# A one-core decoder block: the largest top-k search taken off VectorE, two merged operands in slots, the mixer products one block later

## The chip, the cores and the metric

The kernel runs on one core of one Trainium2 chip. The metric is the device time of one execution in microseconds (us). TensorE (PE in the profile) multiplies and transposes, VectorE (DVE), ScalarE (ACT) and GpSimd (POOL) do the elementwise work, and SyncE (SP) issues the DMAs.

## The reference, cut to what matters

One decoder layer on x of 1024 tokens by 1024 features in float32. Three sub-layers follow one another, each between two RMS norms and added to the residual; the change touches the first, the mixer.

```python
proj = h @ w_in          # pool channels | q | k | v | index q, k, weights | two gates
a   = _pool_mixer(u_pool, pool_w, pool_scale) @ w_proj_pool
att = _sparse_attention(q, k, v, q_idx, k_idx, w_idx, rel_bias_table)
merged = sigmoid(g_pool) * a + sigmoid(g_attn) * (att @ w_proj_attn)
return merged @ w_out
```

The pool mixer takes trailing means over 2, 4, 8 and 16 tokens in four groups of 128 channels, minus the token, and multiplies each group by a 128x128 matrix. The sparse attention scores all keys for each query with four small index heads, keeps the 256 best causal keys of each query, and does softmax attention over those in eight heads. Then follow attention over 256 memory tokens and a SwiGLU network of width 2816.

## The kernel before, in words

Tokens come in eight blocks of 128. Every float32 product is done as three products of rounded operands: `split` rounds a tile to its high part on ScalarE and subtracts to get the low part on VectorE (names with h and l, as `h_wq`, `l_wq`). So each weight tile and each operand costs one ScalarE and one VectorE instruction before TensorE can use it.

Nothing is issued in the order in which it is written. A `Recorder` collects all instructions of the program with their dependences, gives each a cost (`_cost`), and `schedule` builds each engine's order by a greedy simulation: at each step, an engine that is free takes the earliest-written instruction among those that are ready, and a hand-over from one engine to another is counted as `HOP` = 190 ns. The engines then run these fixed orders, each instruction behind the one before it. Where the real durations differ from `_cost`, an engine waits at the head of its queue for what the plan took to be ready. Buffers are counted too: 42 slots of 4 KB per partition (tag "b"), 4 load buffers (tag "ld"), 3 raw weight buffers ("wraw"), 2 each for the high and low weights ("whi", "wlo"), 4 single PSUM banks and 2 double ones. Instructions that allocate a slot may not run more than 700 instructions ahead of the oldest one that is still to do.

The stages of the mixer, with their span in the profile, are these. Norm and transposition of x, index projections, and scores of the query blocks 2 to 7 (`do_scores`, to 85 us; blocks 0 and 1 need no choice). The four groups of the pool mixer (`for g in range(4)`, from about 60 us to 137 us): two half products `o_u`, trailing sums on GpSimd (`us`), their difference to the token on VectorE (`pl`), split into `ph` and `pll`, two products `mx` with the group's matrix, split into `mh` and `ml`. Then eight blocks m of 128 columns of the pool gate (`for m in range(KC)`, to 255 us): for each half of the tokens a gate product `o_gp`, a tanh on ScalarE, and the projection `ap` of the four mixer results. Then keys, values, queries (`o_k`, `o_v`, `o_q`, to 367 us), two blocks of the attention gate (`o_ga`), keys and values of the memory (`km`, `vm`, from 388 us), attention unit by unit (`lg`, `pt`, `po`), the output projection `o_pa` of the attention in two halves of the tokens (`proj_attn`, the second half to 708 us), and the product with `w_out` (`y`, from 708 us).

The search for the 256 best keys (`topk`) is a bitwise search for a threshold, 32 rounds long. In a round each query block (384 to 1024 keys wide) is compared with its current threshold and counted in one VectorE instruction (`tja`, output bf16, with a sum); then two small instructions on all blocks' counts (`reja`, `canda`) give the next threshold. After the last round, each block needs seven VectorE instructions (`gt`, `left`, `eq`, `pre`, `eq`, `gt`, `mask`) for the exact mask. `topk` is a generator: `tick` moves it on by a third of a round's blocks or so from places in the loops over pool groups, gates, keys, queries, and `tick(1000)` behind the memory's keys and values writes what is left. That sets only the place in the written order, so the rank among ready instructions.

`proj_attn` writes the merged halves to DRAM (`mgd`) through load buffers `gt`; `merged(b)` reads a block of 128 tokens back into a load buffer `mg` and splits it into `mgh` and `mgl` for `y`. The first two blocks' operands `ym` are written behind the whole second half of `proj_attn`.

Of the kernel before, what the change touches and what calls it, by code (L numbers as in the profile page):

```python
# [10 lines left out]
F32 = mybir.dt.float32  # L11
F32R = mybir.dt.float32r
# [5 lines left out]
P = 128  # L18
S = 1024
# [34 lines left out]
class Recorder:  # L54
# [130 lines left out]
    def _cost(self, eng, name, args, kw):  # L185
        n = self._free(args[0])
        src = args[1] if len(args) > 1 and self._is_ap(args[1]) else args[0]
        big = max(n, self._free(src))
        if name == "dma_start":
            a = args[0]  # L190
            total = 1
            for st, c in list(a.ap):
                total *= c
            return (60.0 if eng == "sync" else 1000.0), total * 4 / 360.0
        if eng == "tensor":
            if name == "transpose":
                return 109.0, 0.0
            return n * 0.43 + 7.0, 0.0
        if eng == "scalar":
            return 150 + 0.89 * big + (190 if kw.get("accum_out") is not None else 0), 0.0  # L200
        if eng == "vector":
            ps = any(self.tiles.get(a.tensor.name, [""])[0].startswith("ps") for a in args if self._is_ap(a))
            fast = name in ("tensor_copy", "tensor_scalar", "tensor_single_scalar") and not ps
            if kw.get("accum_out") is not None:
                return 280 + 1.05 * big, 0.0
            return 130 + (0.56 if fast else 1.06) * big, 0.0
        if name == "tensor_scalar":
            return 195 + 1.0 * n, 0.0
        if name == "tensor_copy":
            return 60 + 3.4 * n, 0.0  # L210
        if name == "memset":
            return 60 + 1.0 * n, 0.0
        if kw.get("op") == OP.pow:
            return 464.0, 0.0
        return 60 + 2.1 * n, 0.0
# [125 lines left out]
def hybrid_block_kernel(ctx: ExitStack, tc: tile.TileContext, x, mem, norm_mix_pre, norm_mix_post,  # L341
# [12 lines left out]
    def slot(shape, dt, name):  # L354
        return nc.tile(sb, shape, dt, name=name, tag="b", bufs=NSLOT)
# [286 lines left out]
                                fill=LOW, base=0, channel_multiplier=1)  # L642


    def topk(blocks, tag):
        nb = len(blocks)
        cnt = nc.tile(sb, [P, nb], F32, name=f"cnt{tag}", tag=f"cnt{tag}")
        rej = nc.tile(sb, [P, nb], I32, name=f"rej{tag}", tag=f"rej{tag}")
        cand = [nc.tile(sb, [P, nb], I32, name=f"cand{tag}{j}", tag=f"cand{tag}{j}") for j in range(2)]
        for rnd in range(32):  # L650
            cur = cand[rnd % 2]
            for a, i in enumerate(blocks):
                n = (i + 1) * P
                thr = 0.0 if rnd == 0 else cur[:, a:a + 1].bitcast(F32)
                junk = nc.tile(sb, [P, S], BF, name=f"tj{tag}{rnd}{i}", tag="bf", bufs=2)
                nc.vector.tensor_scalar(junk[:, :n], score[i][:, :n], thr, None, op0=OP.is_ge, op1=OP.add,
                                        accum_out=cnt[:, a:a + 1])
                if a % 3 == 2:
                    yield
            bit = -1 if rnd == 0 else 1 << (31 - rnd)  # L660
            nxt = 1 << (30 - rnd) if rnd < 31 else 0
            nc.vector.tensor_scalar(rej, cnt, float(TOPK), float(bit), op0=OP.is_lt, op1=OP.mult)
            if rnd == 0:
                nc.vector.tensor_single_scalar(cand[1], rej, nxt, op=OP.bitwise_xor)
            else:
                nc.vector.scalar_tensor_tensor(cand[(rnd + 1) % 2], rej, nxt, cur,
                                               op0=OP.bitwise_xor, op1=OP.bitwise_xor)
        fin = cand[0]
        for a, i in enumerate(blocks):
            n = (i + 1) * P  # L670
            thr = fin[:, a:a + 1].bitcast(F32)
            sc = score[i]
            gt = nc.tile(sb, [P, S], BF, name=f"gt{i}", tag="bf", bufs=2)
            nc.vector.tensor_scalar(gt[:, :n], sc[:, :n], thr, None, op0=OP.is_gt, op1=OP.add,
                                    accum_out=cnt[:, a:a + 1])
            left = small([P, 1], F32, f"left{i}")
            nc.vector.tensor_scalar(left, cnt[:, a:a + 1], -1.0, float(TOPK), op0=OP.mult, op1=OP.add)
            eq = nc.tile(sb, [P, S], BF, name=f"eq{i}", tag="bf", bufs=2)
            nc.vector.tensor_scalar(eq[:, :n], sc[:, :n], thr, None, op0=OP.is_equal)
            pre = slot([P, S], F32, f"pre{i}")  # L680
            nc.vector.tensor_tensor_scan(pre[:, :n], eq[:, :n], eq[:, :n], 0.0, op0=OP.add, op1=OP.max)
            nc.vector.scalar_tensor_tensor(eq[:, :n], pre[:, :n], left, eq[:, :n], op0=OP.is_le, op1=OP.mult)
            nc.vector.scalar_tensor_tensor(gt[:, :n], eq[:, :n], -1.0, gt[:, :n], op0=OP.add, op1=OP.add)
            nc.vector.tensor_scalar(mask(i), gt[:, :n], -NEG, None, op0=OP.mult)
            yield

    bg = {"gen": None}

    def tick(n=1):
        for _ in range(n):  # L690
            if bg["gen"] is not None and next(bg["gen"], "end") == "end":
                bg["gen"] = None

    for i in range(2, NB):
        do_scores(i)
    bg["gen"] = topk([2, 3, 4, 5, 6, 7], "a")


    rc = nc.tile(sb, [P, 16], F32, name="rc", tag="rc")
# [2 lines left out]
    pwr = wload(pool_w.rearrange("g c d -> c g d"), "pw")  # L702
    pwh, pwl = slot([P, 4, P], F32R, "pwh"), slot([P, 4, P], F32R, "pwl")
    split(pwh, pwl, pwr)
    mixh, mixl = [], []
    for g in range(4):
        w = WINDOWS[g]
        wh, wl = wcols(w_in, C_POOL + g * P, f"wu{g}", keep=True)
        uu = slot([P, S], F32, f"uu{g}")
        for h in range(2):  # L710
            o = gemm_half(wh, wl, hT, h, f"u{g}", (0, 512) if g or h else (0, 256, 512))
            nc.scalar.activation(uu[:, h * 512:(h + 1) * 512], o, AF.Copy)
            tick(1)
        a, st = uu, 1
        while st < w:
            b_ = slot([P, S], F32, f"us{g}{st}")
            nc.gpsimd.tensor_copy(b_[:, :st], a[:, :st])
            nc.gpsimd.tensor_tensor(b_[:, st:], a[:, st:], a[:, :S - st], op=OP.add)
            a, st = b_, st * 2
        nc.gpsimd.tensor_tensor(a[:, :w], a[:, :w], rc[:, :w], op=OP.mult)  # L720
        nc.gpsimd.tensor_scalar(a[:, :w], a[:, :w], float(w), None, op0=OP.mult)
        pl = slot([P, S], F32, f"pl{g}")
        nc.vector.scalar_tensor_tensor(pl, a, 1.0 / w, uu, op0=OP.mult, op1=OP.subtract)
        ph, pl_ = slot([P, S], F32R, f"ph{g}"), slot([P, S], F32R, f"pll{g}")
        split(ph, pl_, pl)
        mh, ml = slot([P, S], F32R, f"mh{g}"), slot([P, S], F32R, f"ml{g}")
        for h in range(2):
            s = slice(h * 512, (h + 1) * 512)
            o = bank([P, 512], f"mx{g}{h}")
            mm3(o, pwh[:, g], pwl[:, g], ph[:, s], pl_[:, s], True, True)  # L730
            split(mh[:, s], ml[:, s], o, scale=pscale[:, g:g + 1])
        mixh.append(mh)
        mixl.append(ml)


    span = 383
# [26 lines left out]

    mAd = nc.tile(dr, [KC, P, S], F32, name="mAd", tag="mAd", dram=True)
    sAd = nc.tile(dr, [KC, P, S], F32, name="sAd", tag="sAd", dram=True)
    for m in range(KC):
        if m % 2 == 0:
            v = w_proj_pool.rearrange("(k p) n -> p k n", p=P)[:, :, m * P:(m + 2) * P]
# [2 lines left out]
        mA = slot([P, S], F32, f"mA{m}")  # L771
        for h in range(2):
            s = slice(h * 512, (h + 1) * 512)
            o = gemm_half(wh, wl, hT, h, f"gp{m}")
            nc.scalar.activation(mA[:, s], o, AF.Tanh, scale=0.5)
            o2 = bank([P, 512], f"ap{m}{h}")
            cs = slice((m % 2) * P, (m % 2 + 1) * P)
            for c in range(4):
# [253 lines left out]
    for k, (u, nxt) in enumerate(zip(units, units[1:] + [None])):  # L1032
# [4 lines left out]
            attn_gate(k + GFIRST - 1)  # L1037
        for m in PROJ.get(k, ()):
            proj_attn(0, [m], wide=k == 15)
    proj_attn(1, range(KC))  # L1040


    x1d = nc.tile(dr, [S, D], F32, name="x1d", tag="x1d", dram=True)
    x2d = nc.tile(dr, [S, D], F32, name="x2d", tag="x2d", dram=True)
    def merged(b):
        mg = nc.tile(sb, [P, KC, P], F32, name=f"mg{b}", tag="ld", bufs=LD)
        nc.sync.dma_start(mg, mgd[:, :, b * P:(b + 1) * P].rearrange("k d t -> d k t"))
        mgh, mgl = slot([P, KC, P], F32R, f"mgh{b}"), slot([P, KC, P], F32R, f"mgl{b}")
        split(mgh, mgl, mg, scale=0.5)
        return lambda c: (mgh[:, c], mgl[:, c])  # L1050

    ym = [merged(b) for b in range(2)]
    wo = [wsplit(wload(w_out[c * P:(c + 1) * P, :], f"wo{c}"), f"wo{c}", keep=True) for c in range(KC)]
    g2, g3 = gain(norm_mix_post, "g2"), gain(norm_mem_pre, "g3")
    h2T = QuartT("h2")
# [365 lines left out]
```

## Time and profile before

| | us |
|---|---|
| median of three runs (lowest, highest) | 1581.72 (1580.98, 1583.4) |
| the profiled execution | 1580.3 |
| its span on the core | 1578.5 |

Mean granted clock of the profiled execution: 0.996 of full speed. TensorE is busy over 1540.6 us of the span, VectorE over 1100.4, ScalarE over 594.7, GpSimd over 214.9. A busy time is the union of the instructions' spans; a matmul's recorded span is longer than the distance to the next one's start, so a stretch in which TensorE is fully busy can still be slow, and the granted clock has to be read beside it.

### The profile page before, as it was taken

To read this page: it belongs to the slowest core of one execution; us is meant where nothing else is said; L and a number is where in the kernel's file an instruction comes from. 1 tells how busy PE (TensorE), PEld (TensorE's weight loads), DVE (VectorE), ACT (ScalarE), POOL (GpSimd) and SP (SyncE) were. 2 spreads that over 40 slices of the span, in tenths; PEclk is the share of its full clock that TensorE was granted. 3 is DMA by queue.
4 is the path that set the end of the run, shared out by engine and by line. 5 is a ranking of instruction groups with operands and counts; after the bars stand their busy time and mean duration, and the time that the engine had idled before them with its cause. 6 is when DMAs were issued, how large, how long until landed. Compare 5 with 4: busy or idle time off the path is not lost.

```text
span 1578.5 us, 20510 instructions
## 1 busy us (share of the span) xinstructions
PE 1540.6 (98%) x7458; PEld 1294.1 (82%) x7458; DVE 1100.4 (70%) x1848; ACT 594.7 (38%) x991; POOL 214.9 (14%) x311
## 2 busy tenths in 40 slices
PE   6999999999999999999999999999999999999998
PEld 6877888887888888887799887888888888888886
DVE  5699888889743686556865676776677776665545
ACT  6532111222443565324545663222222331464431
POOL 6055000001122442001212220000000000000002
PEclk9999999999999999999999999999999999999999
DMA  7322412453833222489973527644444443786654
GB/s 223 72 67 64 130 54 67 124 183 127 247 101 94 81 74 81 138 273 353 387 272 124 205 83 276 213 157 161 166 164 162 154 153 127 245 292 195 219 175 160
DMA packets 213781, 262.20 MB, mean 166 GB/s; under 512 B 11944, under 2 KB 144816, under 8 KB 213680
## 3 DMA queue, kind: packets, MB, share of 16 engines
q1 hardware_dynamic: 213680, 260.89, 50.6%
q8 instruction: 59, 0.97, 0.3%
q14 instruction: 42, 0.34, 0.1%
HBM read 177.47 MB, written 83.63 MB: 165 GB/s over the span
## 4 chain that ended last, share of the span: by engine, by line
PE 83%; DVE 7%; issue 3%; DMA 3%; ACT 2%; POOL 1%; SPq 0%; DVEq 0%; POOLq 0%; ACTq 0%
PE gb L139 11%; PE gc L139 8%; PE ga L139 7%; PE dB L139 6%; PE o_q L139 5%; PE y L139 5%; PE o_gp L139 5%; PE o_ga L139 4%; PE dA L139 4%; PE o_pa L139 4%; PE dC L139 3%; PE po L139 3%; PE lg L139 3%; PE qm L139 3%; PE z L139 3%
## 5 line engine op out<-in xcount | busy, mean ns | idle before, releaser
L139 DVE TENSOR_SCALAR_CACHE_REDUCE tja<-score,canda 128x384 bf16<-128x384 f32 (+1 forms) x186 | 165.5, 941 | 0.8
L139 DVE TENSOR_TENSOR dlP<-drP,dhP 128x1024 fp32r<-128x1024 f32 x77 | 93.8, 1224 | 49.7 <-ACT dhP L139 27.7
L139 ACT ACTIVATE dhP<-drP 128x1024 fp32r<-128x1024 f32 x77 | 81.6, 1061 | 73.7 <-DMA drP<-wdnT 22.6
L139 POOL TENSOR_SCALAR mef<-ms,ms 128x1 f32<-128x1 f32 x8 | 3.8, 472 | 611.0 <-ACT jf L139 610.7
L139 POOL TENSOR_SCALAR L<-L,ri 128x256 f32<-128x256 f32 (+7 forms) x64 | 47.9, 751 | 162.1 <-DVE ri L139 143.6
L139 ACT ACTIVATE h<-s 128x1024 fp32r<-128x1024 f32 x44 | 45.7, 1056 | 63.1 <-DVE s L139 25.9
L139 PE MATMUL lg<-kTh,qq 128*128 128x512 f32 (+2 forms) x192 | 59.1, 353 | 0.8 <-DVE nn L139 0.8
L139 DVE TENSOR_TENSOR l<-s,h 128x1024 fp32r<-128x1024 f32 x44 | 53.6, 1218 | 5.0 <-PE gc L139 4.8
L139 DVE CUSTOM_DVE_ANT_0 L<-lg,mb 128x256 f32<-128x256 f32 (+1 forms) x64 | 25.1, 400 | 44.9 <-PE lg L139 42.6
L139 DVE TENSOR_TENSOR T<-pt,T 128x512 fp32r<-128x512 f32 x72 | 47.6, 685 | 12.5 <-ACT T L139 12.4
L139 PE MATMUL po<-T,Vh 128*128 128x512 f32 x144 | 54.4, 407 | 1.3 <-DVE T L139 0.8
L139 PE MATMUL y<-h_wo,mgh 128*128 128x512 f32 x128 | 50.9, 398 | 2.4 <-ACT mgh L139 2.4
L139 ACT ACTIVATE T<-pt 128x512 fp32r<-128x512 f32 x72 | 40.4, 595 | 33.4 <-PE pt L139 32.9
L139 POOL TENSOR_TENSOR mb<-Bn,mask 128x1024 f32<-128x1024 f32 (+1 forms) x16 | 33.5, 2092 | 138.9 <-DVE gt L139 115.6
L139 PE MATMUL o_ga<-hTh,h_wga 128*128 128x512 f32 x128 | 50.2, 392 | 1.4 <-DVE Vml__670 L139 1.4
L139 PE MATMUL dB<-dhP 128*128 128x512 f32 x132 | 51.3, 389 | 0.0
L139 PE MATMUL dB<-dlP,dhP 128*128 128x512 f32 x132 | 51.3, 389 | 0.0
L139 PE MATMUL dB<-dhP,dlP 128*128 128x512 f32 x132 | 51.3, 389 | 0.0
L139 PE MATMUL y<-h_wo,mgl 128*128 128x512 f32 x128 | 49.9, 396 | 1.4 <-DVE mgl L139 1.4
L139 PE MATMUL y<-l_wo,mgh 128*128 128x512 f32 x128 | 50.6, 395 | 0.0
L139 PE MATMUL o_pa<-ath,h_wpa 128*128 128x512 f32 x128 | 50.5, 395 | 0.0
L139 PE MATMUL o_pa<-ath,l_wpa 128*128 128x512 f32 x128 | 50.2, 392 | 0.0
(429 smaller groups left out, 4824.8 us busy)
## 6 DMA issues: line engine op xcount, KB each, us to landing
uw<-unitd SPq DMA_DIRECT2D x28, 512.0 KB, 7.0
r_wg<-in_w_gate_up_dram SPq DMA_DIRECT2D x22, 512.0 KB, 5.6
r_wu<-in_w_gate_up_dram SPq DMA_DIRECT2D x22, 512.0 KB, 5.5
r_wdr<-in_w_down_dram SPq DMA_DIRECT2D x22, 512.0 KB, 4.2
wdnT<-r_wdr SPq DMA_DIRECT2D x44, 256.0 KB, 4.5
actS<-gv SPq DMA_DIRECT2D x44, 256.0 KB, 4.8
drP<-actS SPq DMA_DIRECT2D x44, 256.0 KB, 3.8
drP<-wdnT SPq DMA_DIRECT2D x44, 256.0 KB, 4.3
```

The lines of the kernel that those rows point to most:

```text
L139: op.emit = lambda: fn(*args, **kw)
```

## The change

It has three parts and a new price in the planner.

- The search over query block 7 (1024 keys) leaves the common `topk` generator and becomes a second one, tag `c`, with `side=True`, added behind the gate block m = 1. In it a round is: a GpSimd compare into a bf16 tile of a new tag `bp` with one buffer, a ScalarE copy of that tile onto itself with a sum, then the two small VectorE instructions for this block alone. `tick` now moves on every generator in the list `bg`. The planner's price of a GpSimd `tensor_scalar` with bf16 output goes from 195 + 1.0 n to 195 + 2.6 n ns. In the finals `gt` and `eq` move from the two bf16 buffers (`bf`) into one slot (`ge`).
- `mix(g)`, the two products `mx` of a pool group and their splits, is written behind the next group's work, and `mix(3)` behind both gate halves of m = 0.
- The two merged operands `mg0` and `mg1` go into slots rather than load buffers, and `ym` is written between m = 4 and m = 5 of the second half of `proj_attn`.

```diff
         if name == "tensor_scalar":
-            return 195 + 1.0 * n, 0.0
+            return 195 + (2.6 if args[0].dtype == BF else 1.0) * n, 0.0
...
-    def topk(blocks, tag):
+    def topk(blocks, tag, side=False):
+
+        eng = nc.gpsimd if side else nc.vector
...
+                if side:
+                    junk = nc.tile(sb, [P, S], BF, name=f"tj{tag}{rnd}{i}", tag="bp", bufs=1)
+                    nc.gpsimd.tensor_scalar(junk[:, :n], score[i][:, :n], thr, None, op0=OP.is_ge)
+                    nc.scalar.activation(junk[:, :n], junk[:, :n], AF.Copy, accum_out=cnt[:, a:a + 1])
+                    continue
...
-                if a % 3 == 2:
+                if a in (2, 4):
                     yield
...
+            if side:
+                yield
...
-            gt = nc.tile(sb, [P, S], BF, name=f"gt{i}", tag="bf", bufs=2)
+            ge = slot([P, 2, S], BF, f"ge{i}")
+            gt, eq = ge[:, 0], ge[:, 1]
...
-    bg["gen"] = topk([2, 3, 4, 5, 6, 7], "a")
+    bg.append(topk([2, 3, 4, 5, 6], "a"))
...
+        pooled.append((ph, pl_))
+        if g:
+            mix(g - 1)
...
+            if m or not h:
+                gates(m, h, wh, wl, mA)
+            if m + h == 0:
+                gates(m, 1, wh, wl, mA)
+                mix(3)
...
         if m == 1:
             bias_strip()
+            bg.append(topk([7], "c", True))
...
-        mg = nc.tile(sb, [P, KC, P], F32, name=f"mg{b}", tag="ld", bufs=LD)
+        mg = (slot([P, KC, P], F32, f"mg{b}") if b < 2 else
+              nc.tile(sb, [P, KC, P], F32, name=f"mg{b}", tag="ld", bufs=LD))
...
+    proj_attn(1, range(5))
     ym = [merged(b) for b in range(2)]
+    proj_attn(1, range(5, KC))
```

## Rows read from the trace of the kernel before

**Rows 1.** The first part of the page: busy us of each engine, its share of the span, and instructions.

```profile
PE 1540.6 (98%) x7458; PEld 1294.1 (82%) x7458; DVE 1100.4 (70%) x1848; ACT 594.7 (38%) x991; POOL 214.9 (14%) x311
```

**Rows 2.** The view by stretches: a stretch in us, its length, the busy us of PE, weight loads, DVE, ACT and POOL (with instructions), the granted TensorE clock, the DMA share and GB/s.

```profile
79.00:100.00 21.00, 20.45 (x90) 16.62 (x89) 20.59 (x29) 10.94 (x13) 9.88 (x9) 1.00 0.20 51
100.00:120.00 20.00, 18.89 (x83) 15.32 (x83) 19.77 (x35) 5.18 (x7) 10.82 (x12) 1.00 0.28 79
120.00:140.00 20.00, 19.23 (x83) 15.13 (x82) 19.60 (x37) 7.17 (x10) 18.12 (x33) 1.00 0.00 1
160.00:200.00 40.00, 40.00 (x178) 33.11 (x178) 34.67 (x76) 6.89 (x9) 0.00 (x0) 1.00 0.39 119
...
320.00:362.00 42.00, 42.00 (x195) 34.94 (x194) 37.13 (x81) 10.35 (x16) 0.00 (x0) 1.00 0.51 168
362.00:391.00 29.00, 29.00 (x139) 24.41 (x139) 28.41 (x39) 6.01 (x9) 7.46 (x3) 1.00 0.33 110
391.00:402.00 11.00, 5.97 (x37) 5.77 (x36) 10.86 (x13) 1.98 (x3) 0.00 (x0) 0.69 0.47 149
...
708.00:720.00 12.00, 9.62 (x36) 7.48 (x35) 8.70 (x9) 6.49 (x7) 0.00 (x0) 0.86 0.90 319
720.00:790.00 70.00, 68.65 (x323) 56.90 (x323) 54.40 (x60) 34.16 (x51) 15.34 (x22) 1.00 1.06 374
```

**Rows 3.** The view of waits, for TensorE over the whole span: tile waited with, engine and tile waited for, us in total, times, the longest.

```profile
PE pt_n L139 <- DVE xn_n L139: 11.7, 4, 8.6
PE km L139 <- DVE l_wkm L139: 5.0, 1, 5.0
PE y L139 <- ACT mgh L139: 2.4, 1, 2.4
PE mx L139 <- ACT ph L139: 1.7, 2, 1.1
PE o_ga L139 <- DVE Vml__670 L139: 1.4, 1, 1.4
PE y L139 <- DVE mgl L139: 1.4, 1, 1.4
...
PE ap L139 <- ACT mh L139: 0.5, 1, 0.5
...
PE ap L139 <- DVE ml L139: 0.3, 1, 0.3
```

**Rows 4.** The timeline of VectorE from 388 us: start us, us, engine, operation and tiles.

```profile
389.73 2.02 DVE L139 TENSOR_TENSOR_SCAN pre<-eq 128x896 f32<-128x896 bf16 x1
...
394.10 0.39 DVE L139 TENSOR_SCALAR mask<-gt 128x896 bf16<-128x896 bf16 x1
394.41 1.27 DVE L139 TENSOR_SCALAR_CACHE_REDUCE gt<-score,canda 128x1024 bf16<-128x1024 f32 x1
...
395.61 1.22 DVE L139 TENSOR_TENSOR l_wkm<-r_wkm,h_wkm 128x1024 fp32r<-128x1024 f32 x1
```

**Rows 5.** The same for ScalarE (366 to 392 us; in brackets the idle time before, and what ended it), and one row of VectorE's.

```profile
366.80 1.06 ACT L139 ACTIVATE h_wga<-r_wga 128x1024 fp32r<-128x1024 f32 x1 [4.62 <-PE o_q L139]
...
377.73 1.06 ACT L139 ACTIVATE h_wkm<-r_wkm 128x1024 fp32r<-128x1024 f32 x1 [4.67 <-PE o_ga L139]
...
388.56 1.06 ACT L139 ACTIVATE h_wkm<-r_wkm 128x1024 fp32r<-128x1024 f32 x1 [4.62 <-PE o_ga L139]
...
368.06 1.20 DVE L139 TENSOR_TENSOR l_wga<-r_wga,h_wga 128x1024 fp32r<-128x1024 f32 x1
```

**Rows 6.** The view by stretches again, for the two places at which TensorE starts after an idle stretch.

```profile
396.88:400.46 3.58, 3.58 (x16) 3.58 (x17) 3.58 (x5) 0.00 (x0) 0.00 (x0) 0.50 0.59 179
...
714.50:718.10 3.60, 3.60 (x9) 2.83 (x10) 2.94 (x3) 1.12 (x2) 0.00 (x0) 0.53 1.04 407
```

**Rows 7.** The chain of work that ended last, from 702 us: start us, us, what.

```profile
702.25 5.81 DMA mgd<-gt
...
708.08 5.29 DMA mg<-mgd
...
713.39 1.06 ACT mgh L139
...
714.50 1.92 PE y L139 x4
```

**Rows 8.** Groups of VectorE instructions between 150 and 362 us, by shape: count, then busy us, mean ns of one, idle before.

```profile
L139 DVE TENSOR_TENSOR l_wq<-r_wq,h_wq 128x1024 fp32r<-128x1024 f32 x8 | 9.8, 1221 | 5.5 <-ACT h_wq L139 5.5
...
L139 DVE TENSOR_TENSOR l_wgp<-r_wgp,h_wgp 128x1024 fp32r<-128x1024 f32 x5 | 6.1, 1220 | 0.0
L139 DVE TENSOR_SCALAR reja<-cnta 128x6 int32<-128x6 f32 x26 | 4.3, 166 | 0.3
L139 DVE SCALAR_TENSOR_TENSOR canda<-reja,canda 128x6 int32<-128x6 int32 x26 | 4.3, 164 | 0.7
```

**Rows 9.** Groups of GpSimd and ScalarE instructions over the whole span, by shape, nearest to the new ones.

```profile
L139 POOL TENSOR_SCALAR L<-L,ri 128x1024 f32<-128x1024 f32 x8 | 9.0, 1128 | 18.3 <-DVE ri L139 9.2 <-PE lg L139 9.1
...
L139 POOL TENSOR_TENSOR l_wki<-r_wki,h_wki 128x1024 fp32r<-128x1024 f32 x3 | 8.0, 2679 | 2.9 <-ACT h_wki L139 2.9
...
L139 ACT ACTIVATE j_na<-za 128x1024 bf16<-128x1024 f32 x8 | 8.5, 1057 | 12.5 <-DVE za L139 12.5
...
L139 ACT ACTIVATION_READ_ACCUMULATOR L<-L,nn 128x1 f32 x48 | 9.3, 194 | 0.0
```

**Rows 10.** Timelines of VectorE and GpSimd side by side from 119 us, and at 382 us.

```profile
119.88 1.27 DVE L139 TENSOR_SCALAR_CACHE_REDUCE tja<-score,canda 128x1024 bf16<-128x1024 f32 x1
121.08 0.08 DVE L139 DVE_READ_ACCUMULATOR tja<-score,canda 128x1 f32 x1
...
122.22 1.86 DVE L139 TENSOR_SCALAR reja<-cnta 128x6 int32<-128x6 f32 x1
...
124.31 0.61 DVE L139 TENSOR_SCALAR_CACHE_REDUCE tja<-score,canda 128x384 bf16<-128x384 f32 x1
...
121.36 2.68 POOL L139 TENSOR_TENSOR us<-uu 128x1023 f32<-128x1023 f32 x1 [4.14 <-ACT uu L139]
...
124.29 1.89 POOL L139 TENSOR_TENSOR us<-us 128x1022 f32<-128x1022 f32 x1
...
382.60 3.11 DVE L139 TENSOR_TENSOR l_wkm<-r_wkm,h_wkm 128x1024 fp32r<-128x1024 f32 x1
...
382.02 2.61 POOL L139 TENSOR_TENSOR mb<-Bn,mask 128x1024 f32<-128x1024 f32 x1 [3.63 <-issue]
```

More of the change, by code (lines that the diff above doesn't have):

```diff
@@ L677, in topk @@
             nc.vector.tensor_scalar(left, cnt[:, a:a + 1], -1.0, float(TOPK), op0=OP.mult, op1=OP.add)
-            eq = nc.tile(sb, [P, S], BF, name=f"eq{i}", tag="bf", bufs=2)
             nc.vector.tensor_scalar(eq[:, :n], sc[:, :n], thr, None, op0=OP.is_equal)
@@ L685, in topk @@
             yield
-    bg = {"gen": None}
+    bg = []
     def tick(n=1):
         for _ in range(n):
-            if bg["gen"] is not None and next(bg["gen"], "end") == "end":
-                bg["gen"] = None
+            for g in list(bg):
+                if next(g, "end") == "end":
+                    bg.remove(g)
     for i in range(2, NB):
         do_scores(i)
-    bg["gen"] = topk([2, 3, 4, 5, 6, 7], "a")
+    bg.append(topk([2, 3, 4, 5, 6], "a"))
     rc = nc.tile(sb, [P, 16], F32, name="rc", tag="rc")
@@ L704, in hybrid_block_kernel, with mix @@
     split(pwh, pwl, pwr)
-    mixh, mixl = [], []
+    mixh, mixl, pooled = [], [], []
+    def mix(g):
+        ph, pl_ = pooled[g]
+        mh, ml = slot([P, S], F32R, f"mh{g}"), slot([P, S], F32R, f"ml{g}")
+        for h in range(2):
+            s = slice(h * 512, (h + 1) * 512)
+            o = bank([P, 512], f"mx{g}{h}")
+            mm3(o, pwh[:, g], pwl[:, g], ph[:, s], pl_[:, s], True, True)
+            split(mh[:, s], ml[:, s], o, scale=pscale[:, g:g + 1])
+        mixh.append(mh)
+        mixl.append(ml)
     for g in range(4):
@@ L725, in hybrid_block_kernel @@
         split(ph, pl_, pl)
[L726 to L733, printed above, removed]
+        pooled.append((ph, pl_))
+        if g:
+            mix(g - 1)
     span = 383
@@ L765, in hybrid_block_kernel, with gates @@
     sAd = nc.tile(dr, [KC, P, S], F32, name="sAd", tag="sAd", dram=True)
+    def gates(m, h, wh, wl, mA):
+        o = gemm_half(wh, wl, hT, h, f"gp{m}")
+        nc.scalar.activation(mA[:, h * 512:(h + 1) * 512], o, AF.Tanh, scale=0.5)
     for m in range(KC):
@@ L773, in hybrid_block_kernel @@
             s = slice(h * 512, (h + 1) * 512)
-            o = gemm_half(wh, wl, hT, h, f"gp{m}")
-            nc.scalar.activation(mA[:, s], o, AF.Tanh, scale=0.5)
+            if m or not h:
[3 more added lines that the diff above has]
+                mix(3)
             o2 = bank([P, 512], f"ap{m}{h}")
@@ L1039, in hybrid_block_kernel @@
             proj_attn(0, [m], wide=k == 15)
-    proj_attn(1, range(KC))
-    x1d = nc.tile(dr, [S, D], F32, name="x1d", tag="x1d", dram=True)
-    x2d = nc.tile(dr, [S, D], F32, name="x2d", tag="x2d", dram=True)
     def merged(b):
-        mg = nc.tile(sb, [P, KC, P], F32, name=f"mg{b}", tag="ld", bufs=LD)
+        mg = (slot([P, KC, P], F32, f"mg{b}") if b < 2 else
+              nc.tile(sb, [P, KC, P], F32, name=f"mg{b}", tag="ld", bufs=LD))
         nc.sync.dma_start(mg, mgd[:, :, b * P:(b + 1) * P].rearrange("k d t -> d k t"))
@@ L1050, in merged @@
         return lambda c: (mgh[:, c], mgl[:, c])
+    proj_attn(1, range(5))
     ym = [merged(b) for b in range(2)]
+    proj_attn(1, range(5, KC))
+    x1d = nc.tile(dr, [S, D], F32, name="x1d", tag="x1d", dram=True)
+    x2d = nc.tile(dr, [S, D], F32, name="x2d", tag="x2d", dram=True)
     wo = [wsplit(wload(w_out[c * P:(c + 1) * P, :], f"wo{c}"), f"wo{c}", keep=True) for c in range(KC)]
```

## The prediction

> **What bounds the kernel now.** I read the busy times first. TensorE is busy for 1540.6 of 1578.5 us [rows 1], so the other engines' totals decide nothing, and a change that takes no matmul away can win only TensorE's holes. The waits of TensorE come next [rows 3]: they name the holes and who ends each. Most of the largest, `pt_n` with 11.7 us, lies in the first norm, which the change doesn't touch. The stretches [rows 2] then show where the others lie: 79 to 140 us, where TensorE is busy 58.57 of 61 us; 391 to 402, with 5.97 of 11; 708 to 720, with 9.62 of 12; and a little to 790. From 160 to 391 us there is no hole at all, although VectorE is busy 34.67 of 40 us and at the end 28.41 of 29. The two deep holes cost more than their waits: behind each, the granted clock stands at 0.50 and 0.53 for some 3.6 us [rows 6], TensorE's lower level of 1.2 GHz, after it had stood idle. At half speed 3.4 us do the work of 1.7, so each clock drop costs 1.7 us more.
>
> So the holes within reach are: `km` 5.0 + 1.7 = 6.7 us; `y` behind `mgh` 2.4 + 1.7 = 4.1; `mx` and `ap` 1.7 + 0.5 + 0.3 = 2.5. Two of 1.4 us each, `o_ga` and `y` behind `mgl`, are not aimed at directly. Sum of the first three: 13.3 us.
>
> **Why `km` waits.** TensorE stands behind the low part of the second memory key weight. Its high part was done at 388.56 + 1.06 = 389.62 us [rows 5], but VectorE took it at 395.61: in front of it stood the finals of block 6 and the first of block 7 [rows 4]. Before, in the gate and query stages, such lateness does nothing: ScalarE started a gate weight at 366.80, VectorE had its low part at 368.06 + 1.20 = 369.26, and it came into use when the weight before was through, at about 377.7, when ScalarE gets the next buffer [rows 5]. That is 8.4 us in hand, and a memory key head is much shorter than such a block.
>
> **Part 1, block 7 off VectorE.** Removed: 32 compares of 1024 keys. One holds VectorE from 119.88 to 121.08, so 1.20 us [rows 10]; 32 x 1.20 = 38.4 us. Added: 32 pairs of small instructions, nearest rows `reja` 166 and `canda` 164 ns [rows 8], 32 x 0.33 = 10.6 us. VectorE's net relief is 27.8 us, if nothing else happens to it. The finals stay there (block 7's included).
>
> Added on ScalarE: 32 sums, by the bf16 square of 1024 with its read of the sum 1.06 + 0.19 = 1.25 us [rows 9], 40 us in all. ScalarE is busy 6.89 of 40 us from 160 to 200 and 10.35 of 42 from 320 to 362 [rows 2], so the room is there. It is the wait that matters, because the tanh and the query splits, on which TensorE's banks depend, queue behind a sum that waits for GpSimd.
>
> Added on GpSimd: 32 compares, which no row shows. The one-input f32 `tensor_scalar` of 1024 takes 1.13 us, the dearest 1024-wide instruction there, with two inputs, 2.68 [rows 9]: 36 to 86 us in total, on an engine that does next to nothing from 160 to 362 us [rows 2]. I take the upper end, 2.7, because the planner's new line (195 + 2.6 x 1024 = 2.86 us) sits beside it; if it is really 1.13, the order merely has air in it.
>
> One round is a ring: compare, sum, two small ones, with four hand-overs. The plan counts 2.86 + 1.25 + 0.13 + 0.13 with hand-overs of 3 x 0.19 + 0.06, 5.0 us. Real: 2.7 + 1.25 + 0.33 and hand-overs of about 0.05 (ScalarE's `mgh` to `y`, 714.45 to 714.50 [rows 7]), 4.5 us. So the ring should keep ahead of the order by up to 0.5 us a round, and ScalarE should rarely stand behind it. The search for the other five blocks takes 32 x (5 compares and a pair); the ring of 32 x 4.5 = 144 us fits beside the 230 us until 391, even where it waits for its turn on VectorE.
>
> What block 7 costs elsewhere is VectorE held up by GpSimd. At 121.36 GpSimd began a 2.68 us addition; `reja`, due at 122.22 with 0.17 us, ended at 124.08, just behind it. `l_wkm` at 382.60 took 3.11 instead of 1.22 beside `mb`. But the counting compare of 384 keys at 124.31 took its usual 0.61 beside the next addition [rows 10]. So small threshold instructions and the low parts wait out a GpSimd instruction, the counting compares don't.
>
> The Trainium skill has this as a rule (SBUF — State Buffer, Who interferes with whom): VectorE and GpSimd share a pair of ports under an exclusive lock, taken for a whole instruction by a VectorE instruction with two SBUF inputs or in a two-port mode, not by the `tensor_scalar` that writes its sum. The rows agree with both halves of it (1.86 for 0.17, 0.61 for 0.61). It speaks against the change, as the compares hold that port some 40% of the stage; I price it next from rows.
>
> Per round of VectorE's common search (26 in the 212 us from 150 to 362, so 8.2 us; some 7 after the change) there are one pair and about 0.7 low parts (18 of `l_wq`, `l_wgp` and their like [rows 8]) that can be caught. A compare of 2.7 us covers 0.38 of 7 us and a catch costs half of it: 1.7 x 0.38 x 1.35 = 0.9 us a round, 28 us in all. Bounds: 0 and 32 x 2.7 = 86. My 28 would eat the whole relief. Still I expect `km`'s hole to go, for two reasons: the order is now made with block 7 off VectorE, so the finals are placed about 30 us earlier, among gates and queries where 8.4 us of lateness are free; and VectorE stands idle 5.3 of 40 us there [rows 2], some 30 us over the stage, which takes up the catches. I take 6 of the 6.7 us (bounds 0 and 6.7). The moved bf16 tiles cost no instruction; the slots are hidden by the time at which they are used.
>
> **Part 2, mixer products one block later.** The number of instructions is the same; TensorE gets the next group's 48 matmuls between `ph` and `mx`, and two gate halves in front of the last `mx`. It can reclaim 2.5 us. The compares of block 7 may slip into the gaps of GpSimd's `us` chain, since the planner takes whatever is ready, and delay `pl` by up to 2.7 us a time; the extra block covers several. I take 2 (bounds 0 and 2.5, or -2 if the chain is stretched past that cover).
>
> **Part 3, merged operands in slots.** `mg1` is fetched at 708.08, as the last `mgd` write that held a load buffer lands at 708.06, and ready 6.4 us later [rows 7]. With a slot of its own and an earlier place its fetch needs only first-half results, finished long before. SP's queue gets two 512 KB fetches earlier, ahead of the last projection weights; the DMA share is 0.90 from 708 and 1.06 from 720 us [rows 2], so the 4.1 us are probably not all kept: the `w_out` rows are next in line. I take 3.2 (bounds 0 and 4.1).
>
> **Sum.** 6 + 2 + 3.2 = 11.2 us, less 1 us for new small waits in a reshuffled order (estimate: the size of one of the lesser waits [rows 3]): the profiled execution's 1580.3 goes to 1570.1. It lay 1.4 us below the median of 1581.72, so the prediction is 1571.5. Everything won: 13.3 + 2.8 for the two 1.4 us waits, 1565.6.
>
> **Rivals.**
> - *The port eats the relief.* VectorE reaches the finals as late as before, since the 28 us of catches equal the 27.8 of relief, and `km` still waits. For: rows 10; the plan knows nothing of it. Against: VectorE's idle share, and the order. Left are 2 + 3.2 - 1: 1577.5.
> - *The ring runs behind its plan (slower).* If compare, sum and pair need more than the planned 5.0 us, each round puts ScalarE and VectorE later, with all gates and weights behind them. With my 4.5, a compare of 3.2 us breaks even; beyond it each further 0.1 us makes 3.2 us over 32 rounds. 8.4 us are in hand, so it decides from 3.2 + 8.4 / 32 = 3.5 us on. At 4.0 TensorE loses 32 x 0.8 - 8.4 = 17.2 us on top of the forecast: 1588.7. For: all of it hangs in three in-order queues, and no row shows the instruction. Against: every 1024-wide row of GpSimd is under 2.7 us [rows 9].
> - *`y` is bound by transfers anyway.* The hole moves a few us on to `w_out`, at a DMA share of 1.06; part 3 gives nothing: 1574.7.
> - *The search isn't shortened where it counts* (the change doesn't do what it says): the ring ends last, and its finals fall on `km` in place of the others. Same time as the first rival, 1577.5.
>
> **Chances and range.** Forecast, with `y` only partly won included (1565 to 1577): 0.62. Port or late ring, 1577 to 1581: 0.18. Slower by the ring, 1585 and more: 0.13. The rest, 0.07, is small losses of a new order that cancel the gains (1579 to 1585). A measurement of this kernel can tell some 0.2%, 3.2 us, from no change. Faster by more than that (under 1578.6) takes the forecast and half of the port case: 0.71. Within: 0.16. Slower (over 1584.9): 0.13. The range runs from 1563 (everything won and 3 us by the new order) to 1587, which leaves out the bad end of the ring.
>
> **What would show it.** After the change, `km` shouldn't wait behind `l_wkm`, and the stretch behind it should show a granted clock of 1.00; `mgh` shouldn't stand before `y`, nor `ph` before `mx`. The compare should be 2.5 to 2.9 us, and the round of block 7 at least 4.5. `reja` and low parts should be longer on average from 140 us on. ScalarE's waits behind GpSimd's compares tell the ring: over 1 us each, and the prediction is in danger. It is wrong if TensorE shows holes between 160 and 391 us, where it has none now.

## The result, and the profile after

The changed kernel takes 1574.15 us (median of five runs, 1573.01 to 1576.88); five runs of the kernel before on the same chip have a median of 1583.4 us. The ratio is 0.9948, with a 95% interval of 0.9937 to 0.9960. On the 1581.7 us from which the forecast started that is 8.2 us won (6.3 to 10.0); 10.2 were forecast, against that median. The profiled execution's span went from 1578.5 to 1571.2 us.

In what follows, a ratio is turned into us by 1581.7 us; one part in a thousand is 1.6 us.

The first part of the page of the changed kernel, against [rows 1]:

```profile
PE 1538.3 (98%) x7458; PEld 1291.7 (82%) x7458; DVE 1068.7 (68%) x1848; ACT 630.2 (40%) x1055; POOL 307.1 (20%) x343
```

VectorE has 31.7 us less, ScalarE 35.5 more, GpSimd 92.2 more, and TensorE's busy time changes by 2.3: the work moved, the bound engine kept its own.

The view by stretches of the changed kernel, as in [rows 2] (in front of the granted clock: busy us of PE, weight loads, DVE, ACT, POOL):

```profile
79.00:100.00 21.00, 21.00 (x94) 17.00 (x93) 20.76 (x35) 11.93 (x15) 12.49 (x11) 1.00 0.21 51
100.00:120.00 20.00, 19.87 (x88) 16.17 (x87) 19.04 (x34) 5.76 (x8) 9.84 (x11) 1.00 0.28 79
120.00:140.00 20.00, 19.42 (x85) 15.38 (x83) 19.93 (x43) 6.43 (x10) 19.34 (x13) 1.00 0.08 27
140.00:160.00 20.00, 19.41 (x83) 15.61 (x84) 17.97 (x43) 8.65 (x14) 16.20 (x34) 1.00 0.40 109
160.00:200.00 40.00, 40.00 (x178) 33.15 (x177) 35.03 (x94) 12.73 (x21) 18.06 (x6) 1.00 0.43 124
...
362.00:391.00 29.00, 29.00 (x140) 24.45 (x139) 16.11 (x14) 5.83 (x8) 9.14 (x4) 1.00 0.33 110
391.00:402.00 11.00, 11.00 (x85) 10.63 (x85) 5.67 (x7) 5.32 (x8) 0.00 (x0) 1.00 1.04 325
...
425.00:480.00 55.00, 52.46 (x250) 42.60 (x250) 25.56 (x96) 24.88 (x59) 15.65 (x20) 1.00 0.34 101
...
700.00:720.00 20.00, 18.27 (x80) 14.51 (x79) 10.18 (x10) 7.42 (x7) 0.00 (x0) 1.00 1.04 369
```

The row to look at is 391 to 402: TensorE was busy 5.97 of 11 us at a granted clock of 0.69 [rows 2], and is now busy for all of them at 1.00. In front of it, VectorE's 28.41 us of 29 have become 16.11: the finals no longer stand in front of the memory's keys. From 160 to 391 TensorE has no hole, before or after, though GpSimd now works 18.06 of 40 us. The hole at 700 to 720 has become smaller, and at 425 to 480 a larger one has come.

TensorE's waits in the changed kernel, against [rows 3]:

```profile
PE pt_n L139 <- DVE xn_n L139: 12.1, 4, 8.9
PE mo L139 <- DVE mT L139: 2.0, 2, 1.8
PE lg L139 <- DVE ri L139: 1.8, 2, 1.0
PE y L139 <- ACT h_wo L139: 1.4, 1, 1.4
...
PE mx L139 <- ACT ph L139: 0.7, 1, 0.7
```

`km` is gone from the list, `y` waits for a weight (`h_wo`) in place of the operand (`mgh`), `mx` has 0.7 us left of 1.7, and two waits are new: `lg` 1.8 us in the first attention units, `mo` 2.0 in the memory attention. The three holes that the change aimed at shrank; the new order opened smaller ones elsewhere.

In the kernel before, VectorE's last mask ran at 407.07 us:

```profile
407.07 0.42 DVE L139 TENSOR_SCALAR mask<-gt 128x1024 bf16<-128x1024 bf16 x1
```

In the changed kernel the last mask is done at 375.8 us, 32 us earlier, and the memory key weights come as soon as their high part is there (in brackets VectorE's own idle time before):

```profile
375.38 0.39 DVE L139 TENSOR_SCALAR mask<-ge 128x896 bf16<-128x896 bf16 x1
...
389.44 1.23 DVE L139 TENSOR_TENSOR l_wkm<-r_wkm,h_wkm 128x1024 fp32r<-128x1024 f32 x1 [9.70 <-ACT h_wkm L139]
392.37 1.23 DVE L139 TENSOR_TENSOR l_wkm<-r_wkm,h_wkm 128x1024 fp32r<-128x1024 f32 x1 [1.70 <-ACT h_wkm L139]
```

### The profile page after: what moved, and what is told of

It is laid out like the page before. It is cut to its first block, busy times and chain, and to the rows that moved or that the text cites. A ratio compares the mean times of both kernels' runs of the same rounds, so it can differ in the third digit from the quotient of the medians.

```text
span 1571.2 us, 20668 instructions
## 1 busy us (share of the span) xinstructions
PE 1538.3 (98%) x7458; PEld 1291.7 (82%) x7458; DVE 1068.7 (68%) x1848; ACT 630.2 (40%) x1055; POOL 307.1 (20%) x343
## 4 chain that ended last, share of the span: by engine, by line
PE 87%; DVE 5%; DMA 4%; issue 2%; ACT 1%; POOL 1%; SPq 0%; DVEq 0%; POOLq 0%; ACTq 0%
PE gb L139 11%; PE gc L139 7%; PE ga L139 7%; PE dB L139 6%; PE o_q L139 6%; PE o_ga L139 5%; PE o_gp L139 5%; PE o_pa L139 4%; PE dA L139 4%; PE y L139 4%; PE dC L139 3%; PE po L139 3%; PE lg L139 3%; PE qm L139 3%; PE ap L139 2%; PE z L139 2%
## 5 line engine op out<-in xcount | busy, mean ns | idle before, releaser
L139 DVE TENSOR_SCALAR_CACHE_REDUCE tja<-score,canda 128x384 bf16<-128x384 f32 (+4 forms) x155 | 128.7, 874 | 0.8
L139 POOL TENSOR_SCALAR tjc<-score,candc 128x1024 bf16<-128x1024 f32 x31 | 89.1, 2875 | 92.7 <-DVE reja L139 44.3
L139 DVE TENSOR_TENSOR l<-s,h 128x1024 fp32r<-128x1024 f32 x44 | 53.6, 1220 | 5.0 <-PE gc L139 5.0
L139 ACT ACTIVATE tjc<-tjc 128x1024 bf16<-128x1024 bf16 x32 | 33.7, 1055 | 53.5 <-POOL tjc L139 53.5
```

What stands on the lines that cost most here:

```text
L139: op.emit = lambda: fn(*args, **kw)
```

## The experiments

The ratios are to the kernel before, with runs of it on the same chip. First the three parts by themselves.

**Part 1 alone.** The kernel before with the second generator, the new price and the finals in slots.

> Part 1 alone (block 7 of the search on GpSimd and ScalarE, with the new price and the finals in slots; mixer products and merged operands as before). Theory: it fills TensorE's hole before km, 5.0 us of waiting and 1.7 us of half clock behind it, and little else: 6 to 8 us faster than before, no wait of km for l_wkm, and the hole before y (2.4 us and a clock drop) still there. Rival, luck of the order: any new order moves small waits by several us, so the gain is anywhere from 0 to 12 us and the km wait may be there in another place.

Measured: 1576.8 us, ratio 0.9967 (0.9953 to 0.9981), so 5.2 us won. `km` doesn't wait; `y` does, for `mgh` (2.0 us, then the clock drop), and the new 1.8 us of `lg` behind `ri` come with this part. A little under the 6 to 8 expected, though the interval, 3.0 to 7.4 us, reaches into them. The stretch behind `y`'s wait, columns as above:

```profile
710.70:714.20 3.50, 3.48 (x9) 2.75 (x10) 3.04 (x3) 1.06 (x1) 0.00 (x0) 0.55 1.01 405
```

**Part 2 alone.** The kernel before with `mix(g)` one block later.

> Part 2 alone (mixer products one block later). Theory: at most the 2.5 us of waits of mx and ap between 79 and 140 us, 0 to 2.5 us faster; km keeps its wait of some 5 us and its clock drop. Rival, luck of the order: km's wait changes too and the time moves by over 3 us either way.

Measured: 1579.64 us, ratio 0.9983 (0.9972 to 0.9994), 2.7 us won. The waits of `mx` and `ap` go from 2.5 us to 0.3. `km` still waits for `l_wkm`, 3.9 us rather than the 5 expected, and a clock drop: the theory holds, a little over its upper end of 2.5 us.

**Part 3 alone.** The kernel before with `mg0` and `mg1` in slots, and `ym` written earlier.

> Part 3 alone (two merged operands in slots and fetched earlier). Theory: the wait of y for mgh (2.4 us) and the clock drop behind it (1.7 us) go, and a shorter wait for w_out (1 to 2 us) comes: 2 to 4 us faster, km as before. Rival, y is bound by transfers anyway: under 1 us.

Measured: 1582.19 us, ratio 1.0003 (0.9991 to 1.0015): nothing. The rival is right. TensorE's waits show what became of it:

```profile
PE km L139 <- DVE l_wkm L139: 5.0, 1, 5.0
...
PE y L139 <- ACT h_wo L139: 2.4, 1, 2.4
...
PE o_pa L139 <- DVE l_wpa L139: 1.5, 1, 1.5
```

`mgh`'s 2.4 us are gone, and 2.4 us of waiting for the first-comers of `w_out` (`h_wo`) and 1.5 us for the second half's projection weight (`l_wpa`) stand in their place. The two fetches went out some 30 us earlier (from 674.9 us on, before at 701.8 and 708.1), among the loads of the projection weights, and the first load of `w_out` went out at 698.6 us in place of 693.4.

**Parts 2 and 3, without part 1.**

> The change without part 1. Theory: the parts add up, so this is what parts 2 and 3 give alone, 2 to 6 us faster than before, km's wait of 5 us still there, and the whole change beats it by 4 to 7 us. Rival, luck of the order: the km wait is gone here too, or the time is over 3 us from the sum of the parts.

Measured: 1577.91 us, ratio 0.9975 (0.9963 to 0.9987), 4.0 us won, with `km` waiting 3.9 us. The sum of the two parts alone is 2.7 - 0.5 = 2.2, of all three 7.4 against 8.2 for the whole. Within their intervals of some 2 us, the parts add up.

**The change without part 3.**

> The change without part 3 (merged operands as before). Theory (part 3 only hands y's wait on, to w_out): within 2.5 us of the changed kernel, with y waiting for mgh again (2 to 3 us) and not for h_wo. Rival (part 3 gives its 3.2 us once the other parts are there): 2.5 to 4.5 us slower than the changed kernel.

Measured: 1572.4 us, ratio 0.9935 (0.9922 to 0.9948), 10.3 us won. It is the best ratio of this study, though its interval overlaps the whole change's. Part 3 gives nothing here either, although `y`'s old waits are back:

```profile
PE y L139 <- ACT mgh L139: 2.7, 1, 2.7
PE y L139 <- DVE mgl L139: 2.0, 1, 2.0
```

**Is `y` short of transfers?** The whole change, with four loads of 512 KB that nobody needs for 120 us held back:

```diff
+    nc.ahead = nc.SHORT
     for j in range(4):
         nc.sync.dma_start(f32(KVm[j]), kvd[j])
+    nc.ahead = nc.AHEAD
```

> The whole change, with the four 512 KB loads of the memory's keys and values (used from about 830 us on, issued at 703 to 709) held back: they may run only 200 instructions ahead instead of 700. Theory (y is short of transfers at 700 to 720 us, DMA share 1.04, so the earlier merged operands only moved the wait on to w_out): y's wait for h_wo (1.4 us) and the small ones behind it go, 1 to 3 us faster than the changed kernel. Rival (SP's order or the three raw weight buffers hold w_out back): the wait stays, same time.

Measured: 1574.36 us, ratio 0.9956 (0.9944 to 0.9968), the time of the changed kernel. As expected, the wait for `h_wo` is gone; but the 1 to 3 us expected weren't won, and another wait came:

```profile
PE y L139 <- DVE za L139: 3.7, 1, 3.7
```

`y` now waits for the norm behind the first token block (`za`), which gives its PSUM bank back. So the stage has at least three limits of nearly the same height one behind the other: operand, weight transfer, bank. Taking away the first moved the wait to the second, and easing the second moved it to the third; the bank itself wasn't tried.

**The price of the compare.** The whole change without its first hunk, so that the planner counts 1.22 us for a compare that takes 2.84.

```diff
-            return 195 + (2.6 if args[0].dtype == BF else 1.0) * n, 0.0
+            return 195 + 1.0 * n, 0.0
```

> The whole change, but with the planner's old price for the bf16 compare (195 + 1.0 n = 1.22 us instead of 2.86; the chip's own is 2.84). The order then takes a round of block 7 to be 3.4 us long, while it needs some 4.5. Theory (the ring is bound by its turn on VectorE, where the common search goes first; a round takes 6.6 us in the changed kernel): within 3 us of the changed kernel, 1571 to 1577. Rival (the ring is bound by its own length, so a wrong price puts ScalarE and VectorE 1.1 us later each round): 32 x 1.1 - 8.4 = 27 us slower than the changed kernel, with waits of TensorE between 160 and 391 us.

Measured: 1590.88 us, ratio 1.0058 (1.0045 to 1.0071): 9.2 us slower than the kernel before, 17 slower than the changed one. My theory fell, and the rival is right in kind, with 17 us for its 27. First ScalarE's wait behind the compare, in all, then TensorE's longest new wait:

```profile
ACT tjc L139 <- POOL tjc L139: 101.7, 30, 5.9
...
PE vtr L139 <- ACT vt L139: 10.4, 1, 10.4
```

Then ScalarE's timeline at that place:

```profile
277.91 1.06 ACT L139 ACTIVATE tjc<-tjc 128x1024 bf16<-128x1024 bf16 x1 [4.47 <-POOL tjc L139]
...
285.15 1.06 ACT L139 ACTIVATE tjc<-tjc 128x1024 bf16<-128x1024 bf16 x1 [4.67 <-POOL tjc L139]
286.11 0.19 ACT L139 ACTIVATION_READ_ACCUMULATOR tjc<-tjc 128x1 f32 x1
286.21 0.58 ACT L139 ACTIVATE vt<-o_v 128x512 f32<-128x512 f32 x1
```

and the stretches there:

```profile
240.00:280.00 40.00, 36.42 (x161) 29.83 (x159) 31.58 (x89) 13.98 (x24) 21.46 (x8) 1.00 0.19 53
280.00:320.00 40.00, 33.16 (x141) 27.44 (x142) 34.03 (x76) 13.52 (x23) 16.50 (x9) 0.87 0.27 79
```

A sum that waits for GpSimd stands in front of `vt`, the copy of the value product; TensorE needs it for its transposes and stands idle 10.4 us, behind which the granted clock is 0.55 from 286.4 to 292 us. A part of the rest lies in the mixer, where `mx` waits 5.5 us in all for `ph` and `pll`. In the changed kernel the same sums wait 53.5 us in all, and TensorE has no hole there. All instructions are the same, so it is a matter of the order.

**Twice the GpSimd work per round.** The whole change, and behind each sum two more compares of 512 keys each, into a tile that nobody reads.

```diff
+                    idle = nc.tile(sb, [P, 512], BF, name=f"ti{tag}{rnd}{i}", tag="bq", bufs=1)
+                    for q in range(2):
+                        nc.gpsimd.tensor_scalar(idle, score[i][:, q * 512:(q + 1) * 512], thr, None, op0=OP.is_ge)
```

> The whole change, and behind each of block 7's compares two more on GpSimd, of 512 keys each, into a tile that nobody reads: about 3 us more of GpSimd in each round, while VectorE has its two-input instructions. Theory (VectorE's small threshold instructions and low parts wait for GpSimd only when they meet it; in the changed kernel a compare starts right behind them, so they hardly meet): the time that VectorE loses to GpSimd from 100 to 330 us goes from about 7 us to 25 to 50 us, and the kernel gets 0 to 8 us slower than the changed one. Rival (they don't exclude each other to speak of): VectorE's durations as in the changed kernel, same time.

Measured: 1579.81 us, ratio 0.9990 (0.9981 to 0.9998), 6.6 us slower than the changed kernel. Groups of VectorE instructions from 100 to 330 us, by shape (count, busy us, mean ns of one):

```profile
L139 DVE TENSOR_SCALAR reja<-cnta 128x5 int32<-128x5 f32 x30 | 13.6, 454 | 0.4
...
L139 DVE SCALAR_TENSOR_TENSOR canda<-reja,canda 128x5 int32<-128x5 int32 x30 | 11.3, 378 | 0.8
L139 DVE TENSOR_TENSOR l_wgp<-r_wgp,h_wgp 128x1024 fp32r<-128x1024 f32 x8 | 10.9, 1368 | 1.1 <-ACT h_wgp L139 1.1
L139 DVE TENSOR_TENSOR l_wq<-r_wq,h_wq 128x1024 fp32r<-128x1024 f32 x6 | 8.5, 1419 | 5.3 <-ACT h_wq L139 5.2
```

The same of the changed kernel:

```profile
L139 DVE TENSOR_TENSOR l_wgp<-r_wgp,h_wgp 128x1024 fp32r<-128x1024 f32 x8 | 11.7, 1464 | 0.7 <-ACT h_wgp L139 0.7
L139 DVE TENSOR_TENSOR l_wq<-r_wq,h_wq 128x1024 fp32r<-128x1024 f32 x6 | 7.7, 1284 | 4.8 <-ACT h_wq L139 4.8
L139 DVE SCALAR_TENSOR_TENSOR canda<-reja,canda 128x5 int32<-128x5 int32 x30 | 7.7, 257 | 0.4
L139 DVE TENSOR_SCALAR reja<-cnta 128x5 int32<-128x5 f32 x30 | 6.6, 218 | 0.0
```

Over the undisturbed 166, 164, 1220 and 1221 ns [rows 8], the four groups lose 1.6 + 2.8 + 2.0 + 0.4 = 6.8 us in the changed kernel (2.6 in the kernel before, all of it `reja`), and 8.6 + 6.4 + 1.2 + 1.2 = 17.4 with twice the work. So the engines do hold each other up, and more GpSimd time means more of it, but less than the 25 to 50 expected: 25 of the 30 `reja` now begin while a GpSimd instruction is running, and only 12 of them take over 0.2 us longer for it. And that is not what costs the 6.6 us: TensorE has no hole from 160 to 391 us here either. It has one at 140 to 160, columns as above,

```profile
140.00:160.00 20.00, 16.00 (x60) 11.76 (x60) 18.49 (x45) 5.79 (x9) 17.54 (x38) 0.91 0.26 79
```

where the added compares had slipped in between the last group's `us` sums on GpSimd (`mx` waits 1.9 us for `ph`, `ap` 1.6 for `mh`), and the other lies at `y`, with 3.6 us for `h_wo`.

**Is `km`'s hole only a wrong price?** The kernel before, with the real duration of the running sum of the finals in the planner.

```diff
+            if name == "tensor_tensor_scan":
+                return 170 + 2.06 * n, 0.0
```

> The kernel before with one price mended in the planner: the running sum of the finals at 170 + 2.06 n ns (its durations in the trace) instead of 130 + 1.06 n. Nothing else is changed. Theory (km's hole is there since VectorE is short of time at the finals): the hole stays at 3 us or more, gain under 3 us. Rival (the hole is there only since the order takes the finals to be shorter than they are): km's wait falls under 1 us and the kernel is 5 to 7 us faster than before, as much as moving block 7 gives.

Measured: 1581.77 us, ratio 0.9999 (0.9985 to 1.0013). The wait becomes shorter, but stays:

```profile
PE km L139 <- DVE l_wkm L139: 3.6, 2, 3.1
```

Nothing is won that could be told from no change, so the theory stands as far as this price goes: VectorE has too much to do there, and planning the running sum with its real duration doesn't help. Other orders of the same instructions, or the counting compares' price in the kernel before, weren't tried.

**How much is luck of the order?** The changed kernel with `HOP` at 200 ns in place of 190.

> The changed kernel with one number of the planner altered that means nothing on the chip: a hand-over counted as 200 ns instead of 190. A control for the luck of the order. Theory (the change's gain is km's hole and the mixer's waits, the rest is luck of a few us): km has no wait, the time is within 4 us of the changed kernel (1570 to 1578). Rival (the whole gain of 8 us is luck of one order): 1578 or more, and km waits again.

Measured: 1577.26 us, ratio 0.9968 (0.9957 to 0.9980): 3.2 us slower than the changed kernel by a number that means nothing on the chip, inside the 4 expected. The two intervals just touch. `km` doesn't wait here either. That the hole goes with part 1 isn't luck: `km` waits for `l_wkm` in none of the nine orders of this study that have part 1, and in all five that don't (3.6 to 5.0 us). But a gain of 3 us or less can be the order's, so the sizes of parts 2 and 3 aren't shown one by one, and part 1's 5.2 us is known to some 2 us.

**Two more prices mended, with and without part 3.** VectorE's counting compares at 135 + 1.04 n and the running sum at 170 + 2.06 n; first in the changed kernel, then in parts 1 and 2 alone.

> The changed kernel with two more of VectorE's prices mended in the planner: counting compares at 135 + 1.04 n ns instead of 280 + 1.05 n, the running sum of the finals at 170 + 2.06 n instead of 130 + 1.06 n. A try at a better version. Theory (prices decide where an in-order queue waits; the compare's did): no wait of TensorE between 140 and 410 us, the small waits of mx (0.7) and lg behind ri (1.8) change, 0 to 4 us faster than the changed kernel. Rival (too high a price of the counting compares was the room that takes up VectorE's lateness): slower by 2 us or more, with waits between 100 and 391 us.

Measured: 1572.69 us, ratio 0.9938 (0.9924 to 0.9952), 9.8 us won. `lg`'s wait for `ri` is gone. The theory missed in one point: it had no hole between 140 and 410 us, but `mx` waits 3.1 us for `ph`, and from 140 to 160 us TensorE is busy 18.15 of 20. The 1.6 us over the changed kernel lie inside the intervals.

> Parts 1 and 2 without part 3, with the two mended prices of VectorE. A try at the best version of this study. Theory (part 3 gives nothing, and the prices at most a little): 0.991 to 0.995 of the kernel before, so as fast as the changed kernel or up to 5 us faster, with y waiting for mgh. Rival (the orders differ by luck only, some 2 us either way): anywhere from 0.992 to 0.997.

Measured: 1571.82 us, ratio 0.9946 (0.9928 to 0.9965). The two steps don't add up. Of all versions, four lie between 0.9935 and 0.9948 with overlapping intervals, the changed kernel among them: a version that clearly beats it wasn't found.

## Why the prediction was right, and where its steps were off

*`km`, 6 us.* Right. The stretch shows it directly, and part 1 alone wins 5.2 us. Both of the reasons given hold: the finals moved forward (the last mask ends 32 us earlier, about 30 were forecast), and VectorE's lateness is free among gates and queries, where TensorE has no hole even with twice the GpSimd work. The rival of the port fell with it: VectorE's busy time went down by 31.7 us, so the relief wasn't eaten.

*VectorE held up by GpSimd, 28 us.* This term was mis-sized: 6.8 us by the four groups above, and only 2.2 of them fall beside a compare of block 7; the other 4.4 fall beside the sums `us` of the pool mixer. The number of meetings was right: 32 x 1.7 x 0.38 = 21 were counted on, and 20 of the 74 instructions in the four groups begin while such a compare runs. What a meeting costs was wrong. The prediction took it from GpSimd's additions [rows 10], where `reja` and `l_wkm` waited till about the end, and set half a compare, 1.35 us. Here are two low parts in the changed kernel, each behind its compare:

```profile
186.46 2.84 POOL L139 TENSOR_SCALAR tjc<-score,candc 128x1024 bf16<-128x1024 f32 x1 [3.11 <-DVE canda L139]
188.05 1.23 DVE L139 TENSOR_TENSOR l_wgp<-r_wgp,h_wgp 128x1024 fp32r<-128x1024 f32 x1 [0.35 <-ACT h_wgp L139]
...
299.81 2.84 POOL L139 TENSOR_SCALAR tjc<-score,candc 128x1024 bf16<-128x1024 f32 x1 [3.64 <-DVE canda L139]
300.54 1.46 DVE L139 TENSOR_TENSOR l_wq<-r_wq,h_wq 128x1024 fp32r<-128x1024 f32 x1 [0.46 <-ACT h_wq L139]
```

The first began 1.59 us into the compare and took its usual 1.23 us; the second began 0.73 us into it and lost 0.24. Over the nine kernels of this study that have part 1 it is the same each time, for compares of the usual length: 15 low parts that began in the first 0.92 us of a compare were held until 0.97 us after its start, and 50 that began from 1.03 us on lost nothing (0.01 us at most). So a low part doesn't wait out a compare, and the port is not held against it for 40% of the stage, as the prediction had it.

The order helps as well. VectorE and GpSimd in the changed kernel at 200 us:

```profile
200.78 0.16 DVE L139 SCALAR_TENSOR_TENSOR candc<-rejc,candc 128x1 int32<-128x1 int32 x1
200.90 0.17 DVE L139 TENSOR_SCALAR reja<-cnta 128x5 int32<-128x5 f32 x1
201.10 0.20 DVE L139 SCALAR_TENSOR_TENSOR canda<-reja,canda 128x5 int32<-128x5 int32 x1
201.33 0.61 DVE L139 TENSOR_SCALAR_CACHE_REDUCE tja<-score,canda 128x384 bf16<-128x384 f32 x1
...
201.10 2.84 POOL L139 TENSOR_SCALAR tjc<-score,candc 128x1024 bf16<-128x1024 f32 x1 [3.50 <-DVE reja L139]
208.34 2.84 POOL L139 TENSOR_SCALAR tjc<-score,candc 128x1024 bf16<-128x1024 f32 x1 [4.39 <-DVE reja L139]
```

Block 7's `candc` often gets its turn when the common round ends, next to `reja` and `canda`. So the compare starts as those two run, and is over before the next pair comes; under it lie the counting compares, which don't wait. The rule of the Trainium skill (SBUF — State Buffer, Who interferes with whom), that a counting `tensor_scalar` doesn't take the shared port pair and a two-input instruction does, agrees with that: the 384-key compare beside it takes its usual 0.61 us. How much of the small loss is the order's and how much the short hold's wasn't taken apart; with twice the work, where the pairs do meet GpSimd, `reja` goes from 218 to 454 ns and `canda` from 257 to 378.

*The ring, 4.5 us a round, compare 2.7.* Close. The compare takes 2.84 us as a median (32 of them from 88.2 to 320.6 us), the sum 1.06 + 0.19. A round comes to (320.6 - 122.8) / 30 = 6.6 us, since it waits for its turn on VectorE; at the end, when the common search is over, the compares start 4.65 us apart (311.31, 315.95 and 320.60 us), so the ring's own length was right. The slower rival didn't come with the new price; with the old one TensorE got the hole, and 17 us were lost. One sign of danger was badly chosen: ScalarE's waits behind the compare were to stay under 1 us each, and they are 53.5 us in 23 waits, without a cost to TensorE. The 8.4 us in hand that I had counted for a weight don't hold for an instruction that TensorE needs at once, as `vt`.

*Part 2, 2 us.* Right: 2.7 alone. In the whole, `mx` keeps 0.7, and the holes lie a little later, at 120 to 160 us, where compares stand in between the `us` sums (at 122.8, 129.9 and 136.9 us).

*Part 3, 3.2 us.* This step failed, in favour of the rival that `y` is bound by transfers anyway: 0.5 us lost alone (1.9 either way), and nothing missing without it. I had subtracted 0.9 us for the busy DMA queues, where all of it had to go. In the whole change `y`'s waits are shorter, 1.7 us in place of 3.8, but without part 3 they are 4.7, and the time is no longer.

*New small waits, 1 us.* Too low. `lg` and `mo` have 3.8 us of waits that weren't there. The control measured 3.2 us between two orders of the same program, so this term was the least certain of all, and it had no range of its own.

Put together: 5.2 and 2.7 for the first two parts and nothing for the third are 7.9, and 8.2 were measured for the whole. Without part 3's 3.2 us the forecast's own terms leave 6 + 2 - 1 = 7.0, inside the measured 6.3 to 10.0. The two errors, `y` put too high and the new waits too low, both make the forecast gain too large, so they don't cancel. One thing leans the other way: `o_ga`'s wait of 1.4 us [rows 3], which the forecast hadn't counted, is gone as well. What else made up for them can't be told from the differences between orders and executions, so that the sum came within 2 us is in part luck.

Left open is why the profiled executions sometimes show a clock drop behind a wait and sometimes not (below); it wasn't tried.

## What to carry to other kernels

Where the bound engine is 98% busy, list its holes with what stands in front of each, and credit a change only with those; moving 38 us of work off an engine was worth the 5 us by which it had been late at one place. A ring over three in-order queues cost TensorE nothing between 160 and 391 us with the order planned by its true duration, and 17 us with one price wrong, so measure the new instruction first. What one instruction costs another that it meets is to be read from that very pair too: the additions' price, carried over to the compares, was some ten times too high (1.35 us a meeting, where 2.2 / 20 = 0.11 was measured). Before freeing one limit of a stage, look at the next in line: if a DMA share of 1.0 stands beside the wait, an earlier fetch displaces another one.

## What the runs showed of the hardware that was not expected

A GpSimd compare of 1024 f32 keys with bf16 output takes 2.84 us, 2.5 times the f32 multiplication of the same size with its 1.13 [rows 9], and as long as the dearest two-input instruction. The row nearest by its operands would have been the wrong guide; the prediction's upper end, 2.7, was the right one.

Of these 2.84 us, VectorE's two-input low parts are held up only in the first 0.97, as shown above. `reja`, with one input, is held up there too, and again towards the end: in part 1 alone, those that began 1.86 us into a compare took 1.0 us in place of 0.17.

A wait doesn't always cost TensorE its clock. Behind a hole of 2.7 us at `y` the granted clock stayed at 1.00 in one kernel (the change without part 3):

```profile
707.30:710.30 3.00, 0.30 (x2) 0.00 (x0) 2.81 (x4) 2.03 (x2) 0.00 (x0) 1.00 0.95 278
710.40:714.40 4.00, 4.00 (x18) 3.31 (x19) 2.94 (x3) 1.06 (x1) 0.00 (x0) 1.00 1.01 408
```

while behind 2.0 us at the same place it fell to 0.55 in another (part 1 alone, above). The 1.7 us that the prediction added to each deep hole are therefore not sure to be there in every execution.

Two executions can differ so where the order is the same. The kernel before and part 3 alone have the same order on every engine and queue up to 670 us. Yet the first norm differs; here is the kernel before, then part 3 alone (columns as above):

```profile
30.00:40.00 10.00, 8.70 (x68) 7.97 (x67) 7.06 (x16) 9.02 (x23) 7.18 (x6) 1.00 0.55 134
...
30.00:40.00 10.00, 7.24 (x47) 7.03 (x48) 7.42 (x15) 6.72 (x15) 4.32 (x4) 0.83 0.50 132
```

That is 1.5 us of TensorE's time and 1.7 us of its clock. So up to 3 us between two single traces need not be the order's; the times above are medians. Over 31 executions of the kernel before on one chip the mean granted clock lay between 0.992 and 0.997, and the time between 1587.5 us, at the lowest clock, and 1577.0, at 0.997.
